# RG-LRU block step with the gates of both directions in one run of tanh, then all exp, then all sqrt; scans written into the sqrt buffers; entry loads and adaLN loads moved

## The chip, the cores and the metric

One Trainium2 chip, all 8 cores, one batch element per core; the cores do not talk to each other. The metric is the device time in microseconds (us) of the slowest core.

Executions of this program come in two states. In the fast one all cores have the same mean granted TensorE clock (about 0.945 for this program). In the slow one the cores of one die, or of both, show a lower clock, and the time is some per cent longer. All comparisons here are between fast executions, or between the cores of dies that were not slowed in an execution ("undisturbed dies": all four cores above 0.94). Where a whole kernel had few fast executions, I give the mean span of the cores on its undisturbed dies; in most fast executions that mean is some 7 to 27 us below the time of the slowest core. From die to die its standard deviation is 6 to 12 us for the kernels with four or more such dies, and 20 for one (b5_best). The experiments ran on three chips, on which the kernel before itself had means of 10138.8, 10140.0 and 10150.8 us. So a difference of 10 us or so between means from different chips says nothing.

## The reference, cut to what matters

The network has two layers, each made of SwiGLU half-step, token mixer, SwiGLU half-step. Each sub-layer is modulated by adaLN values (a product of `silu(c)` with a large weight). The mixer of layer 0 is a bidirectional RG-LRU:

```python
def rglru_coeffs(v, wa, ba, wx, bx, lam):
    r = sigmoid(block_diag(v, wa, ba))
    i = sigmoid(block_diag(v, wx, bx))
    log_a = -RG_C * r * softplus(-lam)
    a = exp(log_a)
    mult = sqrt(-expm1(2.0 * log_a))
    return a, mult * i * v

# rglru_mixer, for each direction d (forward, backward):
    a_c, b_c = rglru_coeffs(v_ctx, ...)           # 256 context tokens
    h_c = linear_scan(a_c, b_c, zeros, reverse)
    a_l, b_l = rglru_coeffs(v_lat, ...)           # 2048 latent tokens
    y_lat = y_lat + linear_scan(a_l, b_l, h_end, reverse)
out_lat = (gelu(g_lat) * y_lat) @ w_out
```

Width is 2048, so there are 16 blocks of 128 channels, and each block's scan runs over 256 + 2048 = 2304 tokens. The mixer of layer 1 is a Fourier mixer; its output weight is first "folded" (sums and differences of two halves), which the kernel does on DVE inside an earlier SwiGLU stage.

## The kernel before

Every operation goes through a small scheduler, `S.op(engine, fn, reads, writes)`, that puts semaphore waits where a buffer is reused. Each engine runs its operations in the order of the program text, and the timelines show no overtaking: further down, ACT stands idle for 5.39 us ahead of one tanh with all its later work behind it. So the order below is the order on each engine. (In the profile views PE is TensorE with its matmuls and PEld its weight loads; DVE is VectorE, ACT ScalarE, POOL GpSimd, and SP the engine whose queue issues many of the DMAs. PSUM is the memory that matmuls write and the other engines evacuate.)

The sigmoid is computed as a tanh, so the block needs three activation tables: tanh/gelu, exp, sqrt. `gA` holds the decay, `gB` the input, one pair for each direction. One buffer `gM` is shared by both directions. `proj` are the projections of the *next* block, cut into pieces (`vch`, `gch`) that fill PE's time between gates.

```python
        def expo(c, d):
            if d == 0:
                S.op("act", ... activation(out=gM, in_=gA[d], func=AF.Exp, scale=c2, bias=c2) ...)
            S.op("act", ... activation(out=gA[d], in_=gA[d], func=AF.Exp, scale=c1, bias=c1) ...)
            if d == 1:
                S.op("pool", ... tensor_tensor(out=gM, in0=gA[d], in1=gA[d], op=ALU.mult) ...)

        def scan(c, d):
            S.op("dve", ... gB[d] = gB[d] * gM ...)
            # forward: gH = scan(gA[0], gB[0]);  backward: gB[1] = scan(gA[1], gB[1]), reversed
        # [cut]
        for c in range(KC):
            # [cut]
            g0[0](); g0[1]()                   # forward: context gates, first latent gate
            if c > 0:
                hsum()                         # POOL: sum of both directions of block c-1
            for i in range(3):
                take(vch)
                g0[2 + i]()
            take(vch)
            expo(c, 0)
            pmul(c, 0)
            if not last:
                conv(nx, 0)
            msqrt()
            # [cut: zout]
            take(vch); take(vch)
            g1[0]()                            # backward: context gates
            take(vch); g1[1]()
            take(vch); g1[2]()
            take(gch); g1[3]()
            take(gch); g1[4]()
            scan(c, 0)                         # forward scan, under the backward gates
            take(gch)
            i0 = ada_pe(0); ada_pe(1)          # adaLN products of layer 0
            expo(c, 1); pmul(c, 1)
            take(gch)
            # [cut: conv, ctx_proj, cast of the next block]
            ada_pe(2)
            msqrt()
            # [cut: four more pieces of gch, ada_pe(3), ada_evac]
            scan(c, 1)
            if not last:
                gelu(nx)
```

Ahead of the blocks is the entry: after the last output projection ("y phase") of the first SwiGLU half-step, 16 residual chunks are loaded, updated, written back and normalised. Each chunk has two parts, latent and context:

```python
            for (off, w, src, dst, t0, which) in segs:
                S.dma("sp", f"xr{m}", ... xr[m][:, off:off + w] <- src ...,
                      reads=src.r(m, t0, w), writes=[r_xr[m]])     # the 2nd part waits for the 1st to land
            # [cut]
            S.dma("act", f"xw{m}", ... dst <- x ..., reads=[rx])   # write-back, in the loop
```

The adaLN weights of layer 1 are applied by 72 "tasks" in the SwiGLU stages. A task takes a buffer of the same weight ring as the stage, loads 1 MB, does 32 tiny matmuls, and evacuates with one DVE operation:

```python
    gu_phase(W, 0, 1, TS[0], posts, ada[:36])                            # stage A
    gu_phase(W, 0, 1, TS[1], post_steps(TS[0], 0, 0, 0, 2), ada[36:])    # stage B
    gu_phase(W, 1, 0, TS[0], merge(post_steps(...), fold_w_steps()))     # stage C, with the weight fold
    gu_phase(W, 1, 0, TS[1], post_steps(TS[0], 0, 0, 1, 0))              # stage D
    gu_phase(W, 1, 1, TF[0], posts)                                      # stage E
```

I call these five stages A to E below.

## Time and profile before

| | before |
|---|---|
| median of the first 3 runs | 11378.73 us (two of them slow) |
| fast run among them | 10152.17 us |
| profiled execution (fast) | cores 10128 to 10168 us, mean 10147.9 |
| RG-LRU block period | 51.2 us, 16 blocks |

The median says nothing here: it is a slow run. The change has to be judged against 10152.

The page of the profiled execution, slowest core (core 7): span, busy time of the engines with their share of the span, and the chain of work that ended last by engine.

```profile
span 10168.3 us, 127066 instructions; the slowest of 8 cores (10128.1 to 10168.3 us)
...
PE 8902.2 (88%) x47995; PEld 4352.2 (43%) x47995; DVE 2602.3 (26%) x3573; ACT 2016.4 (20%) x3052; POOL 678.7 (7%) x999
...
PE 82%; DMA 10%; ACT 2%; DVE 2%; issue 2%; SPq 1%; DVEq 0%; ACTq 0%; POOL 0%; POOLq 0%
```

TensorE bounds most of the kernel. Where it does not, a stage table shows it. Windows of core 0: stretch, its length, busy time of each engine (instructions), granted clock, DMA share, GB/s. The stretches are, in order, the RG-LRU stage, stages A, B, C, D.

```profile
core 0: us, PE busy (x) PEld busy (x) DVE busy (x) ACT busy (x) POOL busy (x), PEclk, DMA share, GB/s
2362.00:3316.00 954.00, 660.13 (x3676) 294.10 (x3675) 580.14 (x406) 566.14 (x490) 186.53 (x130) 0.83 0.43 90
3717.00:4358.00 641.00, 639.02 (x3940) 304.59 (x3938) 140.27 (x221) 72.87 (x124) 48.58 (x80) 1.00 0.94 168
4677.00:5317.00 640.00, 637.95 (x3942) 304.32 (x3941) 140.58 (x224) 74.31 (x126) 48.81 (x80) 1.00 0.93 170
5634.00:6246.00 612.00, 610.19 (x2821) 276.25 (x2819) 187.63 (x313) 77.45 (x126) 23.36 (x44) 1.00 0.77 158
6562.00:7174.00 612.00, 610.04 (x2820) 276.26 (x2818) 138.02 (x185) 75.26 (x126) 23.36 (x44) 1.00 0.59 117
```

Read it so: in stages A to D PE is busy for all but 2 us; A and B are 28 us longer than C and D because they hold 36 tasks each (28/36 = 0.8 us a task). Of these five stretches only the RG-LRU stage has idle PE, some 290 us. Its mean granted clock is 0.83; the clock records in the trace show 0.5 around PE's stops in every block. Note for later that stage C already has DMA engines 77% busy at only 158 GB/s, and 188 us of DVE work where D has 138: that is the fold.

Inside a block the timeline (core 7: start, duration, engine, line, operation; in brackets the idle time before it and what ended it) shows the wait that the change is aimed at:

```profile
2886.25 2.31 ACT L875 ACTIVATE gA_45_21847<-gA_45_21847,coef_53 128x2304 f32<-128x2304 f32 x1
...
2888.46 1.19 ACT L778 ACTIVATE vcA_21845<-PS,vecs_43 128x1024 f32<-128x1024 f32 x1
2889.67 1.28 ACT L882 ACT_TABLE_LOAD   x1
...
2890.96 2.22 ACT L882 ACTIVATE gM_21851<-gM_21851,qtb_57 128x2304 f32<-128x2304 f32 x1
2893.20 1.28 ACT L838 ACT_TABLE_LOAD   x1
...
2895.48 1.01 PE L851 MATMUL PS<-vcb_21846,gwr_42_21844 128*128 128x512 bf16 x2 [6.73 <-ACT gB_48_21850 L838]
...
2898.51 4.96 DVE L889 TENSOR_TENSOR_SCAN gH_21856<-gA_45_21847,gB_47_21849 128x2304 f32<-128x2304 f32 x1
...
2908.79 4.04 POOL L878 TENSOR_TENSOR gM_21851<-gA_46_21848 128x2304 f32<-128x2304 f32 x1
```

Between the forward and the backward gates ACT changes tables from tanh to exp, to sqrt, and back to tanh. PE has nothing to do for 6.73 us and starts again at half clock: until about 2900.3 its matmuls of 512 columns come 0.427 us apart, then 0.216. The forward scan stands at 2898.51, *under* the backward gates that PE is already working on. There are five table loads a block.

### The profile page before, as it was taken

The page shows a single profiled execution, that of the slowest core. Times are in us where ns is not written, and L with a number is a line of the kernel's source. Part 1 is how long each engine was busy: PE and PEld are TensorE (multiplying, and loading weights), DVE is VectorE, ACT ScalarE, POOL GpSimd, SP SyncE. Part 2 cuts the span into 40 slices and gives each one's busy share as a digit, 9 for nine tenths or more (in the row PEclk, how much of TensorE's full clock was granted, in tenths as well). Part 3 has the DMA queues.
Part 4 walks back from the last instruction along what each step waited for, and adds up shares of the span by engine and source line. Part 5 has one row for each costly group of instructions (what it writes and reads, how often), then busy time and mean ns, then how long its engine had stood idle before and what let it go on. Part 6 is the DMA issues. An engine that isn't in the chain of part 4 may idle for free.

```text
span 10168.3 us, 127066 instructions; the slowest of 8 cores (10128.1 to 10168.3 us)
## 1 busy us (share of the span) xinstructions
PE 8902.2 (88%) x47995; PEld 4352.2 (43%) x47995; DVE 2602.3 (26%) x3573; ACT 2016.4 (20%) x3052; POOL 678.7 (7%) x999
## 2 busy tenths in 40 slices
PE   2999999995777669999999999999956499999993
PEld 1655555652333324444444444444423144444441
DVE  1112211223666332211221232122224222111102
ACT  1111111123666221111111111111113211110000
POOL 0000000000222000000000000000000000000000
PEclk9999999997898879999999999999977799999997
DMA  8778879885334779968986776655564566566545
GB/s 162 141 127 164 165 134 157 164 155 136 76 74 81 183 176 175 174 122 154 177 163 125 156 167 132 129 125 120 114 167 142 147 134 125 106 131 122 116 92 129
DMA packets 524532, 1407.93 MB, mean 138 GB/s; under 512 B 64408, under 2 KB 194584, under 8 KB 470944
## 3 DMA queue, kind: packets, MB, share of 16 engines
q0 software_dynamic: 152352, 830.83, 49.3%
q1 hardware_dynamic: 366976, 562.68, 19.5%
q8 instruction: 396, 6.49, 0.3%
q10 hardware_dynamic: 4608, 6.29, 0.2%
q14 instruction: 200, 1.64, 0.1%
HBM read 1987.87 MB, written 221.25 MB: 217 GB/s over the span
## 4 chain that ended last, share of the span: by engine, by line
PE 82%; DMA 10%; ACT 2%; DVE 2%; issue 2%; SPq 1%; DVEq 0%; ACTq 0%; POOL 0%; POOLq 0%
PE PS L178 49%; PE PS L593 25%; PE PS L766 4%; PE PS L987 2%; DMA w_34_88<-modw 1%; DMA xl_22_76<-xs 1%; DMA wa_55_21857<-modw 1%; PE PS L851 1%; PE PS L349 1%; PE PS L393 1%; DMA xl_19_73<-xs 0%; DMA xl_22_76<-ys 0%; DMA xl_22_76<-xT 0%; DMA xl_24_78<-xT 0%; ACT gM_21851 L882 0%
## 5 line engine op out<-in xcount | busy, mean ns | idle before, releaser
L408 DVE TENSOR_TENSOR acc_16_70<-acc_16_70,sq_29_83 128x512 f32<-128x512 f32 (+1 forms) x150 | 97.9, 652 | 2006.2 <-ACT sq_29_83 L407 1993.5
L178 PE MATMUL PS<-hb_28966,w_90_28963 128*128 128x512 bf16 x2432 | 532.6, 380 | 0.5 <-ACT acc_16_70 L397 0.5
L178 PE MATMUL PS<-hb_28966,w_88_28961 128*128 128x512 bf16 x2368 | 517.1, 379 | 0.0
L178 PE MATMUL PS<-hb_28966,w_91_28964 128*128 128x512 bf16 x2176 | 476.9, 380 | 3.5 <-DMA w_91_28964<-win 3.5
L178 PE MATMUL PS<-hb_28966,w_89_28962 128*128 128x512 bf16 x2176 | 475.7, 379 | 0.0
L178 PE MATMUL PS<-hb_28966,w_87_28960 128*128 128x512 bf16 x2112 | 461.2, 379 | 0.2 <-issue 0.2
L178 PE MATMUL PS<-hb_90,w_32_86 128*128 128x384 bf16 x2048 | 342.2, 328 | 47.0 <-ACT hb_90 L473 35.1
L178 PE MATMUL PS<-hb_90,w_34_88 128*128 128x384 bf16 x2176 | 363.7, 329 | 11.1 <-DVE mods_2_44 L356 10.9
L178 PE MATMUL PS<-hb_90,w_33_87 128*128 128x384 bf16 x2176 | 362.6, 328 | 0.3 <-issue 0.3
L178 PEld LDWEIGHTS PS<-hb_28966,w_90_28963 128*128 128x128 bf16 x2432 | 237.0, 98 | 285.0 <-issue 2.7
L178 PEld LDWEIGHTS PS<-hb_28966,w_88_28961 128*128 128x128 bf16 x2368 | 230.5, 98 | 276.6 <-issue 1.2
L178 PE MATMUL PS<-hb_90,w_31_85 128*128 128x384 bf16 x2048 | 338.2, 326 | 0.7 <-ACT ev_28_82 L568 0.7
L178 PEld LDWEIGHTS PS<-hb_28966,w_91_28964 128*128 128x128 bf16 x2176 | 212.4, 98 | 258.8 <-issue 5.8
L178 PEld LDWEIGHTS PS<-hb_28966,w_89_28962 128*128 128x128 bf16 x2176 | 212.2, 98 | 255.9 <-issue 2.9
L568 ACT ACTIVATE ev_28_82<-PS 128x512 f32<-128x512 f32 (+1 forms) x266 | 149.0, 560 | 846.2 <-PE PS L178 812.3
L568 ACT ACTIVATE ev_27_81<-PS 128x512 f32<-128x512 f32 (+1 forms) x264 | 147.8, 560 | 840.4 <-PE PS L178 816.1
L568 ACT ACTIVATE ev_26_80<-PS 128x512 f32<-128x512 f32 (+1 forms) x262 | 146.3, 558 | 842.6 <-PE PS L178 817.1
L178 PEld LDWEIGHTS PS<-hb_28966,w_87_28960 128*128 128x128 bf16 x2112 | 205.4, 98 | 245.7 <-issue 0.3
L766 PE MATMUL PS<-hx_19546,wi_39_21841 128*128 128x512 bf16 x1024 | 263.0, 407 | 29.4 <-ACT hx_19546 L951 26.3
L178 PEld LDWEIGHTS PS<-hb_90,w_34_88 128*128 128x128 bf16 x2176 | 213.9, 98 | 154.4 <-issue 16.3
L178 PEld LDWEIGHTS PS<-hb_90,w_32_86 128*128 128x128 bf16 x2048 | 201.1, 98 | 181.6 <-issue 51.7
L178 PEld LDWEIGHTS PS<-hb_90,w_33_87 128*128 128x128 bf16 x2176 | 213.6, 98 | 143.5 <-issue 5.1
(685 smaller groups left out, 12600.4 us busy)
## 6 DMA issues: line engine op xcount, KB each, us to landing
w_90_28963<-win POOLq DMA_DIRECT2D x38, 1024.0 KB, 12.5
w_88_28961<-win POOLq DMA_DIRECT2D x37, 1024.0 KB, 13.2
w_33_87<-win POOLq DMA_DIRECT2D x34, 1024.0 KB, 11.0
w_34_88<-win POOLq DMA_DIRECT2D x34, 1024.0 KB, 10.9
w_89_28962<-win POOLq DMA_DIRECT2D x34, 1024.0 KB, 11.0
w_91_28964<-win POOLq DMA_DIRECT2D x34, 1024.0 KB, 12.3
w_87_28960<-win POOLq DMA_DIRECT2D x33, 1024.0 KB, 11.6
w_32_86<-win POOLq DMA_DIRECT2D x32, 1024.0 KB, 11.2
```

The costliest lines, as they stand in the source:

```text
L178: ins = e.matmul(out, l, r, start=(i == 0), stop=(i == n - 1))
L349: ins = e.matmul(o, w, scb[:, 2 * c:2 * c + 2], start=(c == 0), stop=(c == KC - 1))
L393: ins = e.matmul(sbank(k, h, n), ones[:], acc[:, h * n:(h + 1) * n], start=True, stop=True)
L408: S.op("dve", lambda e: e.tensor_tensor(out=a, in0=a, in1=sb[:, :n], op=ALU.add), reads=[rsq], writes=[r_acc])
L568: S.op("act", lambda e, tb=tb, h=h, k=ks[0]: e.activation(out=tb[:, :n], in_=sbank(k, h, n), func=AF.Silu), reads=[rPS[2 * ks[0] + h]], wr ...
L593: ins = e.matmul(sbank(k, h, n), buf[:, (c - a) * 128:(c - a + 1) * 128], rhs(c, h), start=(c == 0), stop=(c == nk - 1))
L766: ins = e.matmul(sbank(k, b % 2, 512), buf[:, kk * 256 + o:kk * 256 + o + 128], hx[:, kk, b * 512:(b + 1) * 512], start=(kk == 0), stop=(k ...
L851: ins = e.matmul(PS[:, 3072 + h * 512:3584 + h * 512], wg(d, g), vcb[:, lo + h * 512:lo + (h + 1) * 512], start=True, stop=True)
L987: ins = e.matmul(sbank(k, h, 512), buf[:, c * 128:(c + 1) * 128], zt[i][:, c, h * 512:(h + 1) * 512], start=(c == 0), stop=(c == KC - 1))
```

## The change: intent and diff

- **Blocks.** All tanh of both directions, spread over the eight `v` pieces of the next block, then all exp, then all sqrt: three table loads in place of five, no wait between the directions, no POOL square. Each direction has its own `gM`, and the scans write into it; that frees `gH`.
- **Entry.** The write-backs are issued after all chunks instead of inside the loop. The projection weights of block 0 are loaded by a hook inside the last y phase, in the first two slots of its weight ring.
- **adaLN.** The 72 tasks, 36/36 in stages A/B, become 12/18/16/18/8 in A to E.

```diff
         for m in range(KC):
             it.tick()
             k = next_slot()
+            if hook is not None:
+                hook(m)
 # [cut]
-            S.dma("act", f"xw{m}", ... write-back in the loop ...)
 # [cut]
+        for m in range(KC):
+            S.dma("sp", f"xw{m}", ... the same write-back, after the loop ...)
+    def rec_hook(W):
+        def f(m):
+            if m >= KC - 2:
+                W.wr.i = 2
+            if m == KC - 1:
+                for i in range(2):
+                    handover(W.wr.res[i:i + 1], wi.res[i:i + 1])
+                    load_wi(i)
+        return f
 # [cut]
-            def ctxg(d):        # context gates of one direction
+            def ctxg():         # context gates of both directions
 # [cut]
-            if d == 1:
-                S.op("pool", ... gM = gA[d] * gA[d] ...)
 # [cut: the loop over blocks becomes]
+            ctxg()
+            gelu(c, 0)
             if c > 0:
                 hsum()
+            for i in range(8):
                 take(vch)
+                gq[i]()
+                # [cut: gelu(c, 1) at 0; pmul(c, 0), conv(nx, 0), zout(c - 1) at 3]
+            pmul(c, 1)
+            # [cut: conv, ctx_proj, ctx_conv, cast of the next block]
+            for d in range(2):
+                expo(c, d)
+            i0 = ada_pe(0); ada_pe(1)
+            for i in range(8):
+                take(gch)
+                # [cut: ada_pe(2) at 3, ada_pe(3) at 6]
+            ada_evac(i0)
+            for d in range(2):
+                msqrt(d)
+                scan(d)
 # [cut]
-    gu_phase(W, 0, 1, TS[0], posts, ada[:36])
+    gu_phase(W, 0, 1, TS[0], posts, ada[:12])
-    gu_phase(W, 0, 1, TS[1], post_steps(TS[0], 0, 0, 0, 2), ada[36:])
+    gu_phase(W, 0, 1, TS[1], post_steps(TS[0], 0, 0, 0, 2), ada[12:30])
-    gu_phase(W, 1, 0, TS[0], merge(post_steps(TS[1], 0, 1, 0, 2), fold_w_steps()))
+    gu_phase(W, 1, 0, TS[0], merge(post_steps(TS[1], 0, 1, 0, 2), fold_w_steps()), ada[30:46])
-    gu_phase(W, 1, 0, TS[1], post_steps(TS[0], 0, 0, 1, 0))
+    gu_phase(W, 1, 0, TS[1], post_steps(TS[0], 0, 0, 1, 0), ada[46:64])
-    gu_phase(W, 1, 1, TF[0], posts)
+    gu_phase(W, 1, 1, TF[0], posts, [adaln_task(1, i, W) for i in range(128, 144, 2)])
```

## The prediction

> All times are for the fast state (profiled run 10168 us on the slowest core, lowest timed run 10152 us). The median of 11379 us comes from two slow runs.
>
> **What bounds it now.** The page's chain of waits is 82% TensorE. In the stretches the SwiGLU stages have PE 96-100% busy. PE idles mainly in the RG-LRU entry (2361-2500 us; 12% busy in 2400-2500), its 16 blocks (2511-3342; 77% busy), the step after it, and the Fourier stage. The change touches the first two and moves adaLN work.
>
> **RG-LRU blocks.** The timeline gives a period of 51.25 us. Per block PE has about 35.6 us of work (144 matmuls at 0.216 us, context, adaLN), ACT 33.7, DVE 34. PE idles 6.7 us before the backward gates, waiting for ACT; then it runs 4.3 us at half clock (427 ns matmuls, not 216). The Trainium skill, "TensorE: Matmul & The Clock Gate", Part 1, describes this halving after idleness; this trace agrees.
>
> The change:
> - removes two of five table loads (1.28 us each). Basis: the skill's "ScalarE activation tables: per-element evaluation and per-set limits", "Table sets in the compiler and the runtime" (loads placed for the longest run): tanh and gelu in one set, then exp, then sqrt. The trace shows tanh after gelu without a load.
> - removes the 4.04 us POOL square and its wait, adds one exp of 2.31 us.
> - removes the mid-block PE wait: if nothing else bound, about 39 us a block.
>
> But the context tanh of the next block writes gA[1] and gB[1], which the backward scan still reads, and ACT is in order; all four context tanhs stand before every gate. So one serial loop per block: context tanh 1.1, eight gates paced by 2.16 us of PE (18), a half-clock start (about 2, after some 12 us idle), conv and context 2.5, exp 10.5, sqrt 3.5, then multiply 2.56, scan 4.96, multiply 2.56, scan 4.96. Sum (an estimate from trace durations): about 52 us. The old schedule ran the forward scan under the backward gates. The 12 us do not appear: I expect 50-53 us per block, 0 to +15 us in all. The last block: near 56.
>
> **Entry.** Residual loads run one after another (SP's timeline: each waits for the one before to land). They take 6.2 us per chunk beside write-backs and 4.9 without. Write-backs after the loads save about 25 us. Against it: the hook puts the last three column groups of the y phase into the same two weight buffers, two projection weights loading in between; PE stops 5-15 us. Net -12.
>
> **adaLN.** Same work (72 tasks, 0.8 us each), moved out of stretches with DMA share 0.98-1.00. PE lost only 3.5 us to a weight load there: 0 to -4 us.
>
> **Sum:** 10152 - 12 + 8 - 3, about 10146 us; range 10095 to 10195. Chances: faster by over 2% 0.04, within 2% 0.95, slower 0.01.
>
> **What would show it.** Blocks: period, three table loads, ACT's longest wait on the backward scan ahead of a context tanh, PE idle about 12 us once per block. Entry: SP period under 5 us; PE waits for output weights just before. adaLN: no wait on win near 4097 us.
>
> **What would make it wrong.** If the tanh does not wait for the scan, blocks take 39-42 us and the kernel gains 150-190 us. Write-backs could hold up the first gates.

## The result, and the profile after

| | before | after |
|---|---|---|
| fast runs, us | 10152.17, 10151.37 (of 4) | 10189.37 to 10208.95 (4 of 4) |
| median of the 4 runs of the comparison, us | 10765.45 (two slow) | 10199.94 |
| profiled fast execution, mean of 8 cores, us | 10147.9 | 10169.9 |

Ratio of fast runs 1.0047, with a 95% interval from 1.0023 to 1.0071: the same within 2%, on the slower side. (Ratios are the mean time of one kernel's fast runs over that of the other's of the same rounds, so not quite the ratio of the medians.) The time lies 54 us above the prediction, just over the upper end of its range.

```profile
PE 8848.0 (87%) x47358; PEld 4351.5 (43%) x47995; DVE 2597.6 (25%) x3573; ACT 2004.2 (20%) x3036; POOL 615.1 (6%) x983
...
PE 77%; DMA 13%; DVE 4%; issue 3%; ACT 2%; SPq 1%; DVEq 0%; POOL 0%; ACTq 0%; POOLq 0%
```

The page of after (core 0) already tells something: in the chain of work that ended last, DMA went from 10 to 13% and DVE from 2 to 4%, while PE fell. (The two pages are of different cores, and PE's count of matmul records is 637 short of that of weight loads here, so a small part of its fall is records that are missing.)

The same stretches of core 0 after the change (RG-LRU, A, B, C, D):

```profile
core 0: us, PE busy (x) PEld busy (x) DVE busy (x) ACT busy (x) POOL busy (x), PEclk, DMA share, GB/s
2371.00:3338.00 967.00, 619.01 (x3620) 288.07 (x3684) 569.28 (x405) 552.89 (x472) 120.24 (x113) 0.83 0.42 88
3743.00:4363.00 620.00, 614.81 (x3111) 284.85 (x3168) 138.25 (x197) 72.91 (x124) 31.14 (x56) 1.00 0.67 133
4680.00:5306.00 626.00, 620.05 (x3316) 290.13 (x3375) 139.34 (x205) 74.99 (x126) 36.00 (x62) 1.00 0.73 144
5623.00:6276.00 653.00, 625.36 (x3241) 289.66 (x3300) 189.70 (x330) 74.24 (x126) 34.56 (x60) 0.98 0.87 173
6595.00:7221.00 626.00, 620.60 (x3302) 289.96 (x3361) 139.06 (x203) 73.73 (x125) 35.65 (x62) 1.00 0.74 145
```

Stages A, B, D changed by 0.8 us for each task moved. Stage C did not: it got 16 tasks and 41 us on this core.

All cores together, as means over the 8 cores of the two profiled fast executions. A stage runs from its first matmul to the first of the next; the numbers are worked out from the start times in the traces.

| stretch | before | after | difference |
|---|---|---|---|
| last y phase ahead of the RG-LRU (hook) | 233.8 | 248.8 | +15.1 |
| entry: end of y to the first context gate | 148.8 | 131.2 | -17.6 (medians 149.5, 127.8) |
| first context gate to the last block's output | 828.5 | 846.6 | +18.1 |
| from there to the end of the mixer | 382.8 | 377.9 | -4.9 |
| stage A (36 to 12 tasks) | 641.3 | 621.8 | -19.5 |
| stage B (36 to 18) | 640.0 | 625.7 | -14.3 |
| stage C (0 to 16), with the fold | 611.9 | 651.9 | +40.0 |
| stage D (0 to 18) | 612.3 | 626.9 | +14.6 |
| stage E (0 to 8) | 611.7 | 619.0 | +7.3 |
| all else | | | -17 |

The last line is mostly stages whose code did not change: one of the first layer was 7.6 us shorter, the last y phase 5.8; in the last SwiGLU stage two cores of before had 28 us more than the others. Those two (cores 0 and 1) had a granted clock of 0.81 for 161 us there. I explain nothing of the change by these differences. The rows that the change touches sum to +39.

The blocks, core 0, timeline of the end of one and the start of the next:

```profile
2928.28 1.67 PE L778 MATMUL PS<-hx_19548,wi_32_86 128*128 128x512 bf16 x7
...
2928.91 4.96 DVE L897 TENSOR_TENSOR_SCAN gM_49_21855<-gA_45_21851,gB_47_21853 128x2304 f32<-128x2304 f32 x1
...
2933.95 1.28 ACT L851 ACT_TABLE_LOAD   x1 [5.87 <-DVE gM_49_21855 L897]
...
2936.42 4.96 DVE L897 TENSOR_TENSOR_SCAN gM_50_21856<-gA_46_21852,gB_48_21854 128x2304 f32<-128x2304 f32 x1
2941.48 0.47 ACT L851 ACTIVATE gA_46_21852<-PS,hgb_56 128x256 f32<-128x256 f32 x1 [5.39 <-DVE gM_50_21856 L897]
...
2941.85 0.47 ACT L851 ACTIVATE gB_48_21854<-PS,hgb_56 128x256 f32<-128x256 f32 x1
...
2942.46 1.01 PE L863 MATMUL PS<-vcb_21850,gwr_41_21847 128*128 128x512 bf16 x2 [12.51 <-ACT gB_48_21854 L851]
```

The wait in the middle of the block is gone and a longer one stands between blocks. The next block's context tanh writes into `gA[1]` and `gB[1]` (2941.48), which the backward scan was still reading. All four context tanhs stand ahead of every latent gate, so PE has run out of projections by 2929.95 and waits 12.51 us. Both scans now lie in that gap, one after the other, with no gates above them. PE's waits over eleven blocks say the same (engine, line, waited for: us in total, times, longest), first before, then after:

```profile
PE PS L851 <- ACT gB_48_21850 L838: 73.9, 11, 6.7
PE PS L851 <- ACT gB_47_21849 L838: 20.7, 11, 1.9
```

```profile
PE PS L863 <- ACT gB_48_21854 L851: 137.9, 11, 12.8
```

So 8.6 us a block of PE waiting behind context tanhs ((73.9 + 20.7)/11) became 12.5, and the period went from 51.2 to 52.2 us, although two table loads of 1.28 us are gone. Why 1.0 us more and not 3.9? One long stop in place of several also means fewer matmuls after a restart. Worked out from the matmul and clock records of ten blocks (core 7 of each run, mean period 51.2 and 52.4 us): PE idled 11.3 us a block before and 14.5 after, 3.2 more (the 11.3 hold a wait for adaLN weights that is gone after), but it was busy for 38.0 us in place of 39.9, since 4.3 us of it ran at a granted clock of 0.5 in place of 8.1.

The skill page "ScalarE activation tables: per-element evaluation and per-set limits", section "Table sets in the compiler and the runtime", says loads are placed for the longest run; three loads a block, as the prediction took from it, are what this trace has.

The hook, core 0 of after, last column groups of the y phase:

```profile
2335.94 7.31 PE L595 MATMUL PS<-hid_91,w_36_90 128*128 128x384 bf16 x44 [1.07 <-DMA w_36_90<-wout]
...
2354.21 9.30 PE L595 MATMUL PS<-hid_91,w_35_89 128*128 128x384 bf16 x44 [10.96 <-DMA w_35_89<-wout]
```

The last three column groups share two buffers, so each load has to wait for the matmuls of the group before. PE waits 1.07 and 10.96 us (and 0.95 once before these). After the long wait it runs its first dozen matmuls at half clock (0.32 us apart, not 0.16), so that 44 take 9.30 us instead of 7.31.

### The profile page after: what moved, and what is told of

Read it like the earlier page. It is cut to its first block, busy times and chain, and to the rows that moved or that the text cites. A ratio compares the mean times of both kernels' runs of the same rounds, so it can differ in the third digit from the quotient of the medians.

```text
span 10188.0 us, 126258 instructions; the slowest of 8 cores (10148.8 to 10188.0 us)
## 1 busy us (share of the span) xinstructions
PE 8848.0 (87%) x47358; PEld 4351.5 (43%) x47995; DVE 2597.6 (25%) x3573; ACT 2004.2 (20%) x3036; POOL 615.1 (6%) x983
## 4 chain that ended last, share of the span: by engine, by line
PE 77%; DMA 13%; DVE 4%; issue 3%; ACT 2%; SPq 1%; DVEq 0%; POOL 0%; ACTq 0%; POOLq 0%
PE PS L178 45%; PE PS L595 25%; PE PS L778 4%; DMA wfs<-ev_26_80 2%; DMA w_36_90<-modw 1%; DVE gM_50_21856 L897 1%; PE PS L987 1%; DMA wfs<-ev_28_82 1%; DMA xl_22_76<-xs 1%; PE PS L863 1%; DMA wfs<-ev_27_81 1%; PE PS L349 1%; DMA xl_19_73<-xs 1%; PE PS L393 0%; DMA xl_21_75<-xT 0%
## 5 line engine op out<-in xcount | busy, mean ns | idle before, releaser
L178 PE MATMUL PS<-hb_28825,w_90_28822 128*128 128x512 bf16 x2381 | 528.2, 380 | 6.5 <-DVE mods_3_45 L356 2.6
L178 PE MATMUL PS<-hb_28825,w_89_28821 128*128 128x512 bf16 x2315 | 513.5, 380 | 3.7 <-issue 0.5
L178 PE MATMUL PS<-hb_28825,w_88_28820 128*128 128x512 bf16 x2128 | 474.0, 380 | 18.0 <-DVE mods_3_45 L356 14.4
L178 PE MATMUL PS<-hb_28825,w_87_28819 128*128 128x512 bf16 x2127 | 470.5, 379 | 3.3 <-issue 0.4
L178 PE MATMUL PS<-hb_28825,w_91_28823 128*128 128x512 bf16 x2069 | 457.6, 379 | 2.5
L178 PE MATMUL PS<-hb_92,w_36_90 128*128 128x384 bf16 x2176 | 362.2, 328 | 10.1 <-DVE mods_2_44 L356 9.9
L778 PE MATMUL PS<-hx_19548,wi_31_85 128*128 128x512 bf16 x992 | 244.9, 394 | 31.5 <-ACT hcb_19549 L952 26.6
## 6 DMA issues: line engine op xcount, KB each, us to landing
w_89_28821<-win POOLq DMA_DIRECT2D x37, 1024.0 KB, 10.7
w_34_88<-win POOLq DMA_DIRECT2D x32, 1024.0 KB, 11.3
```

What stands on the lines that cost most here:

```text
L178: ins = e.matmul(out, l, r, start=(i == 0), stop=(i == n - 1))
L778: ins = e.matmul(sbank(k, b % 2, 512), buf[:, kk * 256 + o:kk * 256 + o + 128], hx[:, kk, b * 512:(b + 1) * 512], start=(kk == 0), stop=(k ...
```

## The experiments

Ten kernels. They ask: what makes stage C slow, what the parts of the entry are worth, and whether the loop in the blocks closes where I read it.

### 1. a1_ada_old: adaLN tasks back to 36/36

```diff
-    gu_phase(W, 0, 1, TS[0], posts, ada[:12])
+    gu_phase(W, 0, 1, TS[0], posts, ada[:36])
-    gu_phase(W, 1, 0, TS[0], merge(post_steps(TS[1], 0, 1, 0, 2), fold_w_steps()), ada[30:46])
+    gu_phase(W, 1, 0, TS[0], merge(post_steps(TS[1], 0, 1, 0, 2), fold_w_steps()))
 # [cut: stages B, D, E likewise]
```

> The changed kernel with only the layer-1 adaLN tasks put back (36 and 36 in the two SwiGLU stages of layer 0). Theory A (the loss sits in the first SwiGLU stage of layer 1, where the weight fold runs on DVE): that stage falls from 652 us (mean of 8 cores) to 612, the two stages of layer 0 rise from 622 and 626 back to 640, the last but one SwiGLU stage falls by 7; adaLN in sum gives back 27 us, total near 10172. Rival (the loss is in the RG-LRU part alone and the adaLN move is neutral): total stays at 10190 to 10209.

Measured, on undisturbed cores: stage C 612, A and B 640 to 642, E 611.7. Undisturbed dies mean 10149.7 us (6 dies), against 10177.5 of the changed kernel (8 dies): 28 less. These are not means from one chip, so I rest the 28 on the stages: their rows in the table above sum to the same 28. The one fast run was 10167.28. Stage C on core 0:

```profile
5640.00:6252.00 612.00, 607.00 (x2767) 276.38 (x2822) 188.04 (x314) 77.44 (x126) 23.25 (x44) 1.00 0.76 158
```

So moving the tasks costs about 28 us, and the excess sits in stage C.

### 2. a2_no_hook: weights of block 0 loaded after the y phase again

```diff
-    yp(W, T0[2], 0, 0, pre_steps(...) + pre_steps(...), rec_hook(W))
+    yp(W, T0[2], 0, 0, pre_steps(...) + pre_steps(...))
 # in rglru:
+        for i in range(2):
+            handover([W0.wr.res[i]], [wi.res[i]])
+        load_wi(0)
         load_gw(0)
+        load_wi(1)
```

> The changed kernel without the hook in the y phase ahead of RG-LRU (projection weights loaded at the start of the mixer, as before). If the hook stalls PE: that y phase falls from 248.8 to 233.7 us, and the entry (end of y to the first context gate, mean 131 us) grows by at most 5 because one weight load runs beside the residual loads again; total 10 to 15 us lower, near 10187. Rival (the hook pays for itself in the entry, which is where the 18 us shorter entry came from): entry grows by 15 or more and the total stays.

Measured: the y phase back to 233.8 (from 248.8), but the entry up from 127.8 to 139.9 (medians). Fast runs 10190.73 and 10193.89; ratio to before 0.9983, interval 0.9721 to 1.0246, too wide to use. Undisturbed dies 10173.6, 4 less than after. So the hook costs 15 and pays 12 back: the entry is shorter when the weights are already there. That lies between my two expectations (at most 5, or 15 and more). The likely reason is that their 2 MB do not load beside the residual chunks: the first part of the first chunk held up the second for 10.7 us here (median of 8 cores; before 10.9) and for 4.8 in after, which is half of the 12. I did not test the reason by itself.

### 3. b3_xw_act: write-backs in the loop again, hook kept

```diff
             S.op("act", ... activation(out=sv, in_=x, func=AF.Square) ...)
+            S.dma("act", f"xw{m}", ... write-back ..., reads=[rx], ...)
 # [cut]
-        for m in range(KC):
-            S.dma("sp", f"xw{m}", ... write-back ...)
```

> The changed kernel with the residual write-backs put back into the loop on ACT's queue. If write-backs contend with the residual loads: entry (end of y to first context gate) grows from a median of 128 us to 143 or more, last residual load from 81 to 95 or more. If the shorter entry of the changed kernel came from the hook (no weight load beside the residual loads): it stays within 4 us of 128.

Measured: last residual load issued 92.9 us after the end of y instead of 81.4, entry 139.8 instead of 127.8 (medians). So the move of the write-backs is worth 12 us, not the 25 that I had put down, and somewhat less than the 15 that this run's expectation asked for. Together with the hook's 12 that is 24, about the 22 of the whole change (149.5 to 127.8). This is one execution. (The run's total, 10242.46, holds other differences: its stages ahead of the hook ended some 22 us later than in after; I draw nothing from it.)

### 4. c1_swap: the task ahead of the fold step on every engine

The first rival for stage C: DVE is in order, and the task's evacuation stands behind a fold step that waits for DMA. If that is the cause, turning the order round should free it.

```diff
-            it.tick()
             ib.tick()
+            it.tick()
```

> The changed kernel with the two ticks in a SwiGLU stage swapped, so that an adaLN task, with its eviction on DVE, comes before the fold and post steps of the same column group. If PE waits because the eviction stands behind DVE fold steps that wait for DMA: the first SwiGLU stage of layer 1 falls from 652 to between 625 and 635 us. If the stage is slow because DMA is full (share 0.92 against 0.79 before): it stays at 645 to 655.

Measured: stage C 661 to 664 us on the undisturbed die, median of all cores 664.6; it did not get shorter. It is no proof that it got longer either: executions of kernels with the same stage C gave means over 8 cores of 652 (after), 657 (a2_no_hook) and 666 (b3_xw_act), with single cores from 637 to 681. The order of task and fold within a group is not the cause; c3_loadonly below, which has no evacuations of tasks at all, settles it.

### 5. c2_noload and 6. c3_loadonly: which half of a task costs

Both give a wrong result (error 0.236): the 16 tasks of stage C, without their load (they multiply a tile of zeros in its place, with their PE, PSUM and DVE work kept), or with nothing but their load and its ring slot.

```diff
 # c2_noload, in adaln_task
+            skip = l == 1 and 60 <= idx < 92
+            if skip:
+                rb = r_const
+            else:
+                buf, rb, dn = W.wr.next()
+                S.dma("pool", dn, ... load of modw ...)
-                        w = buf[:, ...]
+                        w = zw[:] if skip else buf[:, ...]
```

```diff
 # c3_loadonly, in adaln_task, after the load [cut: mods[1] is set to 0 at the start]
+            if l == 1 and 60 <= idx < 92:
+                return
```

> The changed kernel, but the 16 adaLN tasks of the first SwiGLU stage of layer 1 read a resident zero tile instead of loading weights (wrong result on purpose; PE, PSUM and DVE work as before). If the loads' share of DMA makes the stage slow: 652 us falls to about 625 (612 plus 16 times 0.8). If the PSUM pair and the DVE eviction each task takes do it alone: it stays near 650.

> The changed kernel, but those 16 tasks only load their weights: no matmuls, no PSUM pair, no eviction (wrong result on purpose). If DMA alone makes the stage slow: it stays near 640 (652 less the 13 us of PE work). If the PSUM pair and eviction are needed for the loss: it falls to 612 to 618.

Measured, stage C: without the load 624.5 us, which is 612 + 16 x 0.8; with the load alone 662 us. Windows of stage C, core 0, first c2_noload, then c3_loadonly:

```profile
5617.00:6241.00 624.00, 621.97 (x3304) 288.46 (x3301) 188.49 (x329) 76.73 (x126) 23.26 (x44) 1.00 0.73 155
```

```profile
5619.00:6284.00 665.00, 626.49 (x2822) 279.32 (x2821) 187.91 (x313) 74.15 (x126) 33.92 (x59) 0.97 0.86 171
```

c3_loadonly has the matmuls that before had (2822 in the window, 2821 there), and 53 us more on core 0. The loads alone are enough, and the rest of the task costs no more than its own 0.8 us. (I had expected about 640 for c3_loadonly. Its 662 lies within the 652 to 666 of the unchanged stage C, so the 13 us of PE work that it lacks cannot be seen.) The waits view of stage C shows the way from the load to PE. Before, core 0 (engine, line, waited for: us in total, times, longest), then after, then c3_loadonly, then c2_noload. The first two list the three `ev` buffers one by one, the last two all three together:

```profile
DVE hid_28965 L570 <- PE PS L178: 301.8, 39, 12.3
...
ACT ev_28_82 L568 <- DMA wfs<-ev_28_82: 25.2, 6, 5.6
```

```profile
DVE ev_26_80 L1133 <- DMA wfs<-ev_26_80: 97.9, 14, 12.1
...
ACT ev_28_82 L568 <- DMA wfs<-ev_28_82: 62.8, 6, 16.7
...
PE PS L178 <- DVE mods_3_45 L356: 17.1, 4, 9.7
```

```profile
DVE ev L1136 <- DMA wfs<-ev: 204.0, 30, 14.8
ACT ev L571 <- DMA wfs<-ev: 142.8, 15, 17.8
...
PE PS L178 <- ACT ev L571: 28.4, 8, 6.6
```

```profile
ACT ev L572 <- DMA wfs<-ev: 48.1, 20, 5.4
...
DVE ev L1137 <- DMA wfs<-ev: 1.3, 1, 1.3
```

Summed over the three buffers, DVE and ACT waited for `wfs` writes 7 and 72 us before, 203 and 136 after, 204 and 143 in c3_loadonly, and 1 and 48 in c2_noload.

The fold writes its results to DRAM (`wfs`) from the same three `ev` buffers into which ACT evacuates SwiGLU's PSUM. Before, DVE waited for PE: PE set the pace. After, the fold's loads and writes complete later beside 16 MB of task loads (DMA share 0.87 in place of 0.77; medians from issue to landing on core 0, loads and writes: 7.8 and 6.5 us in c2_noload, 10.1 and 9.2 in c3_loadonly). The `ev` buffers stay occupied, ACT and DVE wait for them, PSUM is evacuated late, and PE stops. That the loads do it is shown by c2 and c3; the path through `ev` is read from these waits, and no run gave the fold buffers of its own to test it. Two things are not the cause: PE never waits for a weight there, and total bandwidth alone does not do it, for stages A and B before ran at a DMA share of 0.94 and lost nothing; they have no fold. The skill page "DMA: Bandwidth & Descriptors", section "Queues, rings and completion order", says that each DMA engine takes turns between the queues that have work, a packet at a time; that fits loads on one queue delaying the fold's transfers on another, but no run here shows the turns themselves.

### 7. a5_ada_shift: spread, but not into the fold's stage

```diff
-    gu_phase(W, 1, 0, TS[0], merge(post_steps(TS[1], 0, 1, 0, 2), fold_w_steps()), ada[30:46])
+    gu_phase(W, 1, 0, TS[0], merge(post_steps(TS[1], 0, 1, 0, 2), fold_w_steps()))
-    gu_phase(W, 1, 0, TS[1], post_steps(TS[0], 0, 0, 1, 0), ada[46:64])
+    gu_phase(W, 1, 0, TS[1], post_steps(TS[0], 0, 0, 1, 0), ada[30:64])
```

> The changed kernel with the 16 adaLN tasks taken out of the first SwiGLU stage of layer 1 (the one with the weight fold) and put into the next stage, so 12/18/0/34/8. Theory A (the tasks cost their own 0.8 us each wherever they are, and the excess of 27 us comes only from loads that meet the fold's loads and writes): fold stage 612 us in place of 652, next stage 627 + 16 x 0.8 = 640 us, total 27 us less than the changed kernel, about 10150 us on undisturbed dies and a ratio to the kernel before of about 1.000 to 1.002. Rival (any stage with spread tasks pays more than their PE time, so 34 tasks in one stage overload it): next stage over 650 us and the total within 10 us of the changed kernel's 10177.

Measured: stage C 611.8; stage D 638 to 641 on the six cores of the profile that were not slowed in that stage, as 612 + 34 x 0.8 = 639 says. Undisturbed dies 10150.9 us (4 dies), 27 less than after. A stage without the fold takes 34 tasks at their own price. The excess belongs to the meeting of loads and fold.

### 8. a3_split_ctx: backward context gates after the forward gates

If the loop of a block closes at the backward scan because all four context tanhs stand first, then it is enough to move two of them.

```diff
-            def ctxg():
+            def ctxg(d):          # one direction, PSUM bank 6 only
 # [cut]
-            ctxg()
+            ctxg(0)
             gelu(c, 0)
 # [cut]
             for i in range(8):
-                take(vch)
+                if i != 4:
+                    take(vch)
                 gq[i]()
 # [cut]
                 if i == 3:
+                    take(vch)
+                    ctxg(1)
```

> The changed kernel with the context gates of the backward direction issued after the forward gates instead of before all gates. Theory (the block period is one loop closed by the backward context tanh waiting for the backward scan): the tanh no longer waits, the loop closes over the forward scan, period falls from 52.35 to about 46 us (45 to 48), total 80 to 105 us lower, near 10105. Rival (the period is set by the sum of ACT work, or by PE restarting cold, not by that wait): period stays within 1.5 us of 52.

Measured: the profile fell in a slow execution (period 54.0 us; in slow cores of a1_ada_old, with the changed kernel's blocks, it was 58.05). The one fast execution was 10134.16 us; its two dies have a mean of 10111.6, which is 66 less than after and 62 less than a2_no_hook (10173.6, same chip). The next run, which contains the same edit, has the period 47.78 us, so 16 x 4.4 = 70 us. The loop did close where I read it.

### 9. b5_best: the pieces that paid, together

The changed kernel with a1_ada_old, a2_no_hook and a3_split_ctx, and one more edit: both parts of a residual chunk in one issue, so that the second does not wait for the first to land.

```diff
-            for (off, w, src, dst, t0, which) in segs:
-                S.dma("sp", f"xr{m}", lambda e, ...: e.dma_start(...), ...)
+            S.dma("sp", f"xr{m}", lambda e: [e.dma_start(...) for (off, w, src, dst, t0, which) in segs], ...)
```

> The changed kernel with adaLN put back, no hook, split context gates, and both parts of a residual chunk issued together instead of the second waiting for the first to land. Block period near 47.5 us (45 to 49) in undisturbed cores, first SwiGLU stage of layer 1 612 us, y phase ahead of the mixer 234 us, last residual load at 60 to 75 us instead of 81 to 93. Total 10050 to 10090 us in the fast state, ratio to the kernel before 0.990 to 0.994. Rival for the residual loads (limited by DMA throughput, not by landing order): last load stays above 80 us and the total is near 10090 to 10110.

Measured: correct; fast runs 10066.39 to 10126.81 (4); ratio to before 0.9935, interval 0.9906 to 0.9964. Last residual load issued 50.9 us after the end of y (after: 81.4), landed 58.5 (after: 83.9), entry 107.7 us (medians). SP's queue, core 3, loads of residual parts, first before, then b5_best:

```profile
2376.83 0.42 SPq L646 DMA_DIRECT2D xr_58_21860<-xT  x1
2380.73 0.33 SPq L646 DMA_DIRECT2D xr_58_21860<-ctxT  x1
```

```profile
2374.47 0.45 SPq L647 DMA_DIRECT2D xr<-xT  x1
...
2374.96 0.44 SPq L647 DMA_DIRECT2D xr<-ctxT  x1
```

Before, 3.9 us pass between the two parts of a chunk, the landing of the first; there, 0.5. None of the other edits in b5_best touches the entry except the hook's removal, so the fair comparison is a2_no_hook: 139.9 there, 107.7 here. This one edit saved 32 us, more than the 22 of the two entry edits of the change together.

In the block, one wait for a scan remains: the *forward* context tanh waits for the forward scan, which is what the loop runs through now (core 3):

```profile
2912.67 1.28 ACT L849 ACT_TABLE_LOAD   x1 [5.88 <-DVE gM L895]
...
2915.05 1.01 PE L861 MATMUL PS<-vcb,gwr 128*128 128x512 bf16 x2 [6.60 <-DVE gB L892]
```

The releaser in PE's line is to be read with care. It names DVE's multiply because that ended 0.01 us before; by the program this matmul waits for the PSUM bank that the context tanhs read, and they ended 0.25 us before. Both start when the forward scan ends, so the reading stands.

### 10. d1_pool_sq: one exp out of that loop

```diff
-            S.op("act", ... activation(out=gM[d], in_=gA[d], func=AF.Exp, scale=c2, bias=c2) ...)
+            if d == 0:
+                S.op("act", ... the same ...)
             S.op("act", ... activation(out=gA[d], in_=gA[d], func=AF.Exp, scale=c1, bias=c1) ...)
+        def square():
+            S.op("pool", ... tensor_tensor(out=gM[1], in0=gA[1], in1=gA[1], op=ALU.mult) ...)
 # [cut]
             ada_pe(1)
+            square()
             for i in range(8):
                 take(gch)
-                if i == 3:
+                if i == 2:
                     ada_pe(2)
-                if i == 6:
+                if i == 4:
                     ada_pe(3)
```

> The previous best version (adaLN tasks as before, no early weight load, backward context gates after the forward gates, both parts of a residual chunk issued together; block period 47.8 us, slowest core about 10066 to 10074 us undisturbed) with two edits in the block: M of the backward direction comes from a square on POOL, about 4 us, in the place of a 2.31 us exp on ACT; and the last two adaLN products are issued earlier. Theory: the block's loop runs through ACT (tanh, four exp, two sqrt) and the forward scan, so the 2.31 us that leave ACT leave the period; it falls to about 45.5 us, 16 blocks give 25 to 37 us, total 10035 to 10060 us, ratio to the kernel before about 0.990. Rival: PE and DVE are nearly tied with ACT (PE idles only about 6.6 us in the block and then runs at half clock; the DVE's first multiply starts at once after the adaLN evacuation), so the period falls by less than 1 us and the total stays within 10 us of 10070.

Measured: correct; period 45.34 us, against 47.78: 2.44 less, for the exp of 2.31. Fast runs 10026.66 and 10039.99; before, on the same chip, 10152.05, 10160.21 and 10171.65. The quotient of these means is 0.987. Undisturbed dies 10013.1 us (8 dies) against 10138.8 for before (10 dies): 1.2% less. So ACT and the forward scan are the loop, and PE and DVE are not yet in the way. (The run holds two edits, and the earlier adaLN products were not tried alone; the drop is the exp's size.) The square costs DVE a little: in the first block the multiply begins after the square's end and takes 2.56 us; in later blocks the two overlap by 0.7 us and it takes 3.08.

```profile
2865.50 4.02 POOL L889 TENSOR_TENSOR gM<-gA 128x2304 f32<-128x2304 f32 x1 [7.01 <-ACT gA L885]
...
2868.86 3.08 DVE L897 TENSOR_TENSOR gB<-gB,gM 128x2304 f32<-128x2304 f32 x1 [1.42 <-ACT gM L893]
```

This is the fastest version that I ran.

## Why the prediction was right or wrong

**Right: "The 12 us do not appear: I expect 50-53 us per block".** The removed work is 12 us a block on paper, and the period came out at 52.2. The mechanism was the one predicted: the context tanh waits for the backward scan, PE stands once a block for about 12 us (12.51 measured), three table loads. a3_split_ctx and b5_best show it by taking the loop away: 47.8. One mark differs a little: ACT's longest wait is the one for the forward scan ahead of the table load (5.87 us), with the one for the backward scan right after it (5.39). The size was a little off: the sum of the loop gave 52 us, but the total was put at +8 for the blocks; from the first context gate to the last output they took 18 more, and the rest of the mixer 5 less.

**Wrong, and decisive: "adaLN. Same work (72 tasks, 0.8 us each) ... 0 to -4 us".** It was +28 (a1_ada_old: 28 less with the tasks put back). The step that failed is that a task costs 0.8 us wherever it is put. That held in A, B, D and E (E: 7.3 us for 8 tasks) and not in C, where 16 tasks took 40 us, 2.5 each. I looked at the stretches that the tasks left, where the DMA share was 0.98 to 1.00 at its peak and PE lost only 3.5 us to a load. I did not ask what else used the DMA queues and the `ev` buffers in the stretches that they went to. There the loads delay the fold's transfers, and those hold the buffers of the evacuation (c2_noload, c3_loadonly; a5_ada_shift avoids C and loses nothing). A high DMA share was not the danger sign; short transfers that an evacuation waits for were, as far as the waits tell. The profile of before already showed them: ACT waited for `wfs` writes in stage C (25 us for one of the three buffers), for free, since PE was not waiting for ACT.

**Wrong in size: "Write-backs after the loads save about 25 us".** b3_xw_act measured 12. The failed step is the cost of a chunk beside write-backs. From the first to the last residual load the changed kernel takes 5.3 us a chunk ((81.4 - 2.5)/15) and b3_xw_act 6.0: 0.8 us a chunk between them, where I had 1.3.

**Right in size, incomplete: "PE stops 5-15 us" for the hook.** The y phase took 15 us longer, at the end of the range (on core 0: stops of 10.96, 1.07 and 0.95 us, and 2 us more for the 44 matmuls after the restart). What was missing is that the hook also frees the entry from two weight loads, 12 us (a2_no_hook). So "Net -12" for the entry came out as -17.6 + 15.1 = -2.5. That it was no further off is partly luck: 13 us too much for the write-backs and 12 us forgotten for the hook work against each other.

**The sum.** Predicted -12 + 8 - 3 = -7; measured in the rows that the change touches -3 + 13 + 28 = +39, of which the profiled executions show +22 because of -17 in stages that did not change. The timed fast runs differ by 48 (10199.94 against 10152), 9 more than the rows. Of the 46 us by which the rows missed, adaLN is 31, the entry 9 and the blocks 5. So the adaLN tasks are two thirds of the miss; without it the time would have been near 10169. The time lies only 5 us above the upper end of the predicted range, so putting any one of the three right would have brought it to that end or below.

What stays open: by what path in the memory system the task loads delay the fold (queue turns, or the DRAM itself), whether `ev` buffers of the fold's own would cure it, and why the same stage C took 652 to 666 us from one execution to another.

## What to carry to other kernels

When work is regrouped by activation table, look for the serial loop that the regrouping builds: the wait in the middle went away here, but both scans lost their cover and the first write of the next block closed the loop; moving two small tanhs behind other work gave back some 66 us that the regrouping alone had not. When background loads are moved, judge the stretch that they go to by its short transfers that hold shared buffers, not by its DMA share or the matmuls' slack. And look at who waits for a landing before reordering transfers: issuing two halves together saved more than moving sixteen write-backs.

## What the Trainium skill lacked or had wrong

- "ScalarE: Activation LUTs", section "What ACT_TABLE_LOAD costs", gives about 1283 ns for the load, which every block here shows (1.28 us), plus a drain of about 1380 ns for every switch. The drain is not seen here: in the first timeline above a load starts at 2889.67 and the sqrt that needed it at 2890.96, and the activation ahead of the load ended at 2889.65 (2888.46 + 1.19). In the 55 loads between 2550 and 3100 us on that core the medians are 0.018 us ahead of the load and 0.012 behind it. A switch costs 1.3 us in this trace, not 2.66.
- "TensorE: Matmul & The Clock Gate", Part 1, advises to budget the 13/16 clock for dense matmuls on all cores (on the default power profile; which one ran here is not on record). Here eight cores run dense matmuls with a granted clock of 1.00 in nearly all SwiGLU stages of the profiled fast executions before, after and b5_best; the exception is 161 us at 0.81 on cores 0 and 1 of before. Otherwise 0.81 was seen in slowed stages (core 4 of d1_pool_sq: 0.81 in its first SwiGLU stage, 567 us, against 470 us on core 0 at 1.00 in the same execution).
- "DMA: Bandwidth & Descriptors", section "Queues, rings and completion order", says how queues take turns, not what loads on one queue cost short transfers on another. Here 16 loads of 1 MB beside the fold made the stage 27 us longer than the tasks' own 13 (27 to 41 in three executions with this stage) at a DMA share of 0.87 and 173 GB/s, while 36 such loads at 0.94 and 168 GB/s without the fold cost nothing beyond their own matmuls.
- "ScalarE: Activation LUTs", section "Table sets: the hidden batching unit", treats the grouping by table as a gain for ACT. I found on no page that it can take the cover from what stood between the groups: five loads to three took 2.6 us of loads out of a block, and its period went from 51.2 to 52.2 us.
